# Hybrid decoder block on one core: the store of the last local attention outputs becomes a step of the latent attention's list scheduler

## The chip, the cores and the metric

The kernel runs on one core of one Trainium2 chip. Its engines are TensorE (PE, and PEld for its weight loads), VectorE (DVE), ScalarE (ACT), GpSimd (POOL) and SyncE (SP). SP only issues transfers here. The metric is the device time of one execution in microseconds; the time of a kernel is the median of its runs.

## The reference, cut to what matters

One layer over 1024 positions of width 1024, in float32:

```python
h = rmsnorm(x, mix_norm_g[l])
proj = h @ w_in[l]
qa, ka, va, q_lat, kv_lat, k_r, g_a, g_b = jnp.split(proj, IN_OFFSETS, axis=-1)
o_a = swa_sink_attention(qa, ka, va, swa_sinks[l])        # 8 heads, window of 128
cq = rmsnorm(q_lat, q_norm_g[l])                          # 384 wide
qb = (cq @ w_uq[l]).reshape(B, S, MLA_HEADS, MLA_QK_DIM)  # 64 plain + 32 rotary a head
ckv = rmsnorm(kv_lat, kv_norm_g[l])                       # 256 wide
kvb = (ckv @ w_ukv[l]).reshape(B, S, MLA_HEADS, MLA_NOPE_DIM + MLA_V_DIM)
o_b = mla_attention(q_nope, q_rope, k_nope, k_rope, vb)   # 8 heads, causal
y = jax.nn.sigmoid(g_a) * (o_a @ w_o_swa[l]) + jax.nn.sigmoid(g_b) * (o_b @ w_o_mla[l])
x = x + y @ w_out[l]
h = rmsnorm(x, ffn_norm_g[l])
x = x + (jax.nn.silu(h @ w_gate[l]) * (h @ w_up[l])) @ w_down[l]
```

A last norm follows.

## The kernel before

Positions are handled in 8 blocks of 128. Every float32 product is made of three matmuls on high and low halves: `mm3` (L263 to L269) multiplies high by high, high by low and low by high. So each operand is split first: ScalarE casts the high half (L260, or L1233 in the stage below), and DVE or POOL subtracts it for the low half (L261, L272).

The stages in order are: the projections; the local attention in 16 steps, with the products of the two gates between (class `Seven`, accumulators `fa` and `fb`); the opening of the latent attention (L1220 to L1457); the latent attention; the output mix; the feed-forward part. This change touches the joint between the local attention and the opening of the latent one.

**The end of the local attention.** `sw_pv(it)` (L1106) makes the output of one step and gathers four steps in a tile `oa` of 128 x 1024 floats (DVE, L1121 and L1122). After every fourth step, L1123 and L1124 store that tile to memory (`oa_d`, 512 KB), from where it is read again late in the latent attention (L1756). The last of the four stores comes from the call at L1203, the last line of the stage.

**The opening of the latent attention.** Its parts are steps of a list scheduler, class `Plan` (L95). A step has an engine, a cost, steps that it comes after, a rank, and the slots that it uses and frees. `run` (L110) keeps a clock for each engine, takes the step that can start first, with the lower rank ahead among those that can start within 30 ns, and emits its instructions; so the costs, ranks and slots set the order in which PE, DVE, ACT and POOL get their instructions. The steps that matter here:

- `c`, `k` (`latent_steps`, L1238): four transposes of the latents `lat` into a PSUM bank `lT`, then the high half (ACT) and the low half (DVE) into `cq` or `ckv`.
- `ld` (`load_steps`, L1295): loads of the raw weights, both parts of `w_uq` and both of `w_ukv`, in a tile `wr` each.
- `a` (`uq_steps`, L1303): the halves of the raw uq weights, in tiles `wuq`; `b` (`ukv_steps`): those of ukv, in `wv`.
- `r`, `ra`, `rj`, `rq`, `rd` (`rope_steps`, L1252): the rotary part of all queries, in two halves s of the positions. PE's product `r`, DVE's products with the tables `rope_cs`, POOL's joins `rr`, the halves `rq` (ACT, POOL) and the stores `rq_d` (L1280). `load_rope` (L1347) reads these rows back into the tiles `qT` of the heads (L1350).
- `x`, `xd`: the rotary keys (`krT`, then `kT`).
- `gm`, `ge` (`gate_steps`, L1352): the last products of the gates and the copies out of their banks; `gs` stores the gates (L1384).
- `Q`: the first query product; after it the latent attention starts, whose scores are `scb`.

The tiles `lat`, `wr`, `wuq`, `rr`, `go` and `oa` come from one pool, `u`, of 21 equal slots. The planner counts these slots: `in_use` (L1453) lists those taken when the opening starts, and each step's `use` and `free` take and return one. In the kernel before, `oa` is not in that list. Which buffer a tile then gets is decided by the pool when the step is emitted, and a tile put into a buffer waits, by semaphore, until the last reader of that buffer is done; for a buffer that a store reads, that is the landing of the store. PSUM banks (`p`, 4, and `w`, 4) are counted in the same way.

SP's queue holds all transfers of this stretch. A transfer whose wait isn't over holds up all behind it.

Of the kernel before, what the change touches and what calls it, by code (L numbers as in the profile page):

```python
# [18 lines left out]
S = 1024  # L19
D = 1024  # L20
NB = S // P
# [168 lines left out]
def hybrid_block_kernel(  # L190
# [29 lines left out]
    nc = tc.nc  # L220
# [23 lines left out]
    def U(name, dt=F32, shape=(P, 1024)):  # L244
        return pool.tile(list(shape), dt, tag="u", name=uid(name))
# [7 lines left out]
    def P1(name, shape=(P, 512)):  # L253
        return ps1.tile(list(shape), F32, tag="ps", name=uid(name))
# [22 lines left out]
    def blk(b, n=1):  # L277
        return slice(b * P, (b + n) * P)
# [27 lines left out]
    oa_d = dram.tile([4, P, 2, 512], F32, name="oa_d")  # L306
# [642 lines left out]
    oa_t = {}  # L949
# [156 lines left out]
    def sw_pv(it):  # L1106
        g, b = divmod(it, NB)
        d = sw.pop(it)
        po = P1("o", (P, 2, 2, P))
        prev = max(b - 1, 0)  # L1110
        steps = [(vv[prev // 4][:, prev % 4, g], 0)] + ([(vd[g][:, b], 1)] if b else [])
        for vst, n in steps:
            nc.tensor.matmul(po, vst, d["ph"][:, n], start=n == 0, stop=False)
            nc.tensor.matmul(po, vst, d["pl"][:, n], start=False, stop=n == len(steps) - 1)
        tmp = U("ot", F32, (P, 2, 2, P))
        nc.scalar.copy(tmp[0:64], po[64:128])
        if b % 4 == 0:
            oa_t[it // 4] = U("oa", F32, (P, 2, 512))
        oa = oa_t[it // 4]
        oc = blk(b % 4)  # L1120
        nc.vector.tensor_tensor(oa[0:64, :, oc], po[0:64, :, 0], tmp[0:64, :, 0], op=ALU.add)  # L1121
        nc.vector.tensor_tensor(oa[64:128, :, oc], po[0:64, :, 1], tmp[0:64, :, 1], op=ALU.add)  # L1122
        if b % 4 == 3:  # L1123
            nc.sync.dma_start(oa_d[it // 4], oa_t.pop(it // 4))  # L1124

    def kv_out(t, r, b):
# [42 lines left out]
    lat = []  # L1169
# [8 lines left out]
    for it in range(N_SW):  # L1178
        if it + 2 < N_SW:
            sw_q(it + 2)  # L1180
        gate_step()
        if it + 1 < N_SW:
            sw_qT(it + 1)
        if it in (0, 5):
            v_sums(it // 5)
        if it in (1, 6):
            v_parts(it // 6)
        gate_step()
        if it + 1 < N_SW:
            sw_scores(it + 1)  # L1190
        if it == N_SW - 1:
            st.load_to(st.index[("uq", 0)])
            load_lat(4)
        if it >= 1:
            sw_pv(it - 1)
        gate_step()
        sw_pT(it)
        if it + 1 < N_SW:
            sw_exp(it + 1)
    gate_step()  # L1200
    load_lat(NB)
    gate_step()
    sw_pv(N_SW - 1)  # L1203
    in_order.__exit__(None, None, None)

# [22 lines left out]
    def pre_step(kind, *key, x, **kw):  # L1228
        pre.add((kind, *key), rank=x + PRANK.get(kind, 0), **kw)
# [209 lines left out]
    for s in range(2):  # L1439
        pre_step("lf", s, x=0, eng="S", cost=1, emit=lambda: None, free=[("lat", 4 * s + b) for b in range(4)],  # L1440
                 after=[("c", j, s) for j in range(3)] + [("k", j, s) for j in range(2)] + [("x", s)])
    before = None
    for key, at in zip((("uq", 0), ("uq", 1), ("ukv", 0), ("ukv", 1)), XS["ld"]):
        load_steps(key, before, at)
# [5 lines left out]
    query_first_steps(XS["q"])  # L1450
    by_pre = tc.manual_schedule(engines={engines.PE, engines.DVE, engines.Activation, engines.Pool})
    by_pre.__enter__()
    in_use = [("lat", b) for b in range(NB)] + ["cos", "sin", ("graw", 0), ("graw", 1), "sum", "pu"]  # L1453
    in_use += [("gw", n) for n in GN if n < gates.n_prep]
    pre.run({"p": 4, "w": 4, "V": V_SLOTS, "U": U_SLOTS}, held=[("U", k, key) for k, key in enumerate(in_use)] + [("p", 3, ("gb", "A", 1))] + [
        ("V", 2 * n + i, ("hq", gates.seq[GN[n]][1], i)) for n in range(len(GN)) for i in range(2)])
# [945 lines left out]
```

## Time and profile before

| what | value |
|---|---|
| median of 3 runs | 1321.35 us (1320.81 to 1322.18) |
| the profiled execution | 1320.95 us |
| its span, first to last instruction | 1319.2 us |
| mean granted TensorE clock | 0.997 |
| moved by transfers | 210.49 MB, mean 160 GB/s |
| last stores of `oa` | issued at 316.40 us of the span |

The profile is one execution. Times in it are microseconds from the first instruction. A row of the timeline has the start, the length, the engine, the line, the operation, the tiles (out<-in), and in brackets the idle time of that engine ahead of it and what released it. "SPq" is SP issuing a transfer; its length is the time to issue it, not to move it. The busy table by stretch has for each engine the busy time and the number of instructions, then the granted clock, the share of the transfer engines' time and GB/s. The chain that ended last goes back from the last instruction, at each step to what released it.

### The profile page before, as it was taken

To read this page: it belongs to the slowest core of one execution; us is meant where nothing else is said; L and a number is where in the kernel's file an instruction comes from. 1 tells how busy PE (TensorE), PEld (TensorE's weight loads), DVE (VectorE), ACT (ScalarE), POOL (GpSimd) and SP (SyncE) were. 2 spreads that over 40 slices of the span, in tenths; PEclk is the share of its full clock that TensorE was granted. 3 is DMA by queue.
4 is the path that set the end of the run, shared out by engine and by line. 5 is a ranking of instruction groups with operands and counts; after the bars stand their busy time and mean duration, and the time that the engine had idled before them with its cause. 6 is when DMAs were issued, how large, how long until landed. Compare 5 with 4: busy or idle time off the path is not lost.

```text
span 1319.2 us, 18715 instructions
## 1 busy us (share of the span) xinstructions
PE 1306.1 (99%) x6463; PEld 1102.4 (84%) x6463; DVE 919.9 (70%) x1514; ACT 643.2 (49%) x1301; POOL 566.4 (43%) x552
## 2 busy tenths in 40 slices
PE   9999999999999999999999999999999999999997
PEld 6899888887888888888888888888888888888886
DVE  7869777765778885589889755766566555663962
ACT  7434666665477787545464322232223323644452
POOL 2116666553333267310134467775566621022520
PEclk9999999999999999999999999999999999999999
DMA  9454332436410022896231336743454335996503
GB/s 375 161 187 154 117 111 85 132 105 211 143 30 17 25 81 81 309 265 191 84 124 49 126 139 222 260 178 133 180 183 162 134 119 201 386 361 225 178 24 134
DMA packets 81246, 210.49 MB, mean 160 GB/s; under 512 B 9408, under 2 KB 16064, under 8 KB 80448
## 3 DMA queue, kind: packets, MB, share of 16 engines
q1 hardware_dynamic: 78416, 202.48, 43.4%
q0 software_dynamic: 1440, 4.72, 1.9%
q10 hardware_dynamic: 1296, 2.10, 0.5%
q8 instruction: 51, 0.84, 0.3%
q14 instruction: 43, 0.35, 0.1%
HBM read 143.34 MB, written 61.73 MB: 155 GB/s over the span
## 4 chain that ended last, share of the span: by engine, by line
PE 96%; DVE 1%; issue 1%; ACT 1%; DMA 1%; POOLq 0%; POOL 0%; SPq 0%; ACTq 0%; DVEq 0%
PE fa L269 8%; PE fa L267 8%; PE fa L268 8%; PE fb L267 6%; PE fb L269 6%; PE fb L268 6%; PE fd L268 5%; PE fd L267 5%; PE fd L269 5%; PE pTb L1580 2%; PE xo L268 2%; PE xo L267 2%; PE xo L269 2%; PE ob L1618 1%; PE scb L1535 1%; PE ob L1617 1%
## 5 line engine op out<-in xcount | busy, mean ns | idle before, releaser
L261 DVE TENSOR_TENSOR wl<-wr,wl 128x512 fp32r<-128x512 f32 x147 | 143.4, 997 | 67.6 <-ACT wl L260 67.2
L261 DVE TENSOR_TENSOR lrv<-lr,lrv 128x1024 fp32r<-128x1024 f32 x77 | 105.1, 1396 | 49.6 <-ACT lrv L260 48.2
L260 ACT CAST lrv<-lr 128x1024 fp32r<-128x1024 f32 x77 | 80.2, 1052 | 95.2 <-PE fd L269 70.7
L267 PE MATMUL fd<-lrv 128*128 128x512 f32 x308 | 119.8, 389 | 0.0
L268 PE MATMUL fd<-lrv 128*128 128x512 f32 x308 | 119.8, 389 | 0.0
L269 PE MATMUL fd<-lrv 128*128 128x512 f32 x308 | 119.8, 389 | 0.0
L260 ACT CAST wl<-wr 128x512 fp32r<-128x512 f32 x147 | 85.2, 620 | 3.6 <-DVE wr L962 1.7
L1564 POOL TENSOR_SCALAR p<-p,denb 128x384 f32<-128x384 f32 (+3 forms) x64 | 47.9, 750 | 86.8 <-DVE denb L1560 72.2
L261 DVE TENSOR_TENSOR wl<-sm,wl 128x512 fp32r<-128x512 f32 x59 | 52.1, 907 | 35.1 <-ACT wl L260 35.0
L275 POOL TENSOR_TENSOR wr<-wr,sm 128x512 f32<-128x512 f32 x20 | 30.5, 1529 | 97.5 <-DVE wl L261 97.5
L267 PEld LDWEIGHTS fd<-lrv 128*128 128x128 f32 x308 | 57.8, 188 | 12.1
L269 PEld LDWEIGHTS fd<-lrv 128*128 128x128 f32 x308 | 57.8, 188 | 12.0
L268 PEld LDWEIGHTS fd<-lrv 128*128 128x128 f32 x308 | 57.8, 188 | 11.9
L397 POOL TENSOR_SCALAR ms<-ss 128x1 f32<-128x1 f32 x32 | 10.4, 324 | 112.8 <-ACT xn L2131 62.8
L2043 ACT ACTIVATE act<-sm 128x512 f32<-128x512 f32 x11 | 7.0, 633 | 104.1 <-DVE sm L272 104.1
L272 DVE TENSOR_TENSOR ptl<-pTb,pth 128x512 fp32r<-128x512 f32 (+2 forms) x96 | 49.5, 548 | 8.7 <-ACT pth L1591 8.4
L275 POOL TENSOR_TENSOR sm<-wr,wr 128x512 f32<-128x512 f32 (+1 forms) x36 | 41.6, 1162 | 30.6 <-PE fb L269 26.1
L1555 ACT ACTIVATE p<-scb,nmb 128x384 f32<-128x384 f32 (+3 forms) x64 | 47.8, 748 | 13.0 <-DVE nmb L1550 9.0
L1550 DVE CUSTOM_DVE_ANT_0 scb<-scb,mask 128x384 f32<-128x384 f32 (+3 forms) x64 | 48.3, 760 | 6.9 <-PE scb L1537 6.3
L267 PE MATMUL fb<-t3h,wl 128*128 128x512 f32 x120 | 48.1, 401 | 0.0
L1591 ACT CAST pth<-pTb 128x512 fp32r<-128x512 f32 (+2 forms) x96 | 43.1, 484 | 9.9 <-PE pTb L1580 9.4
L268 PE MATMUL fb<-t3l,wl 128*128 128x512 f32 x120 | 47.4, 395 | 0.0
(403 smaller groups left out, 4258.1 us busy)
## 6 DMA issues: line engine op xcount, KB each, us to landing
lr<-la_d SPq DMA_DIRECT2D x77, 256.0 KB, 5.4
wr<-in_w_gate_dram SPq DMA_DIRECT2D x22, 512.0 KB, 4.4
wr<-in_w_up_dram SPq DMA_DIRECT2D x22, 512.0 KB, 5.1
la_d<-sd SPq DMA_DIRECT2D x22, 512.0 KB, 5.1
wd<-in_w_down_dram SPq DMA_DIRECT2D x22, 512.0 KB, 6.5
rb_d<-wd SPq DMA_DIRECT2D x22, 512.0 KB, 2.6
lr<-rb_d SPq DMA_DIRECT2D x44, 256.0 KB, 5.4
lr<-in_w_down_dram SPq DMA_DIRECT2D x33, 256.0 KB, 5.4
```

Of the source, the lines that this page charges most:

```text
L260: nc.scalar.copy(hi, src)
L261: (eng or nc.vector).tensor_tensor(lo, src, hi.bitcast(F32), op=ALU.subtract)
L267: nc.tensor.matmul(ps, ah, bh, start=first and i == 0, stop=False, skip_group_check=go_on)
L268: nc.tensor.matmul(ps, ah, bl, start=False, stop=False, skip_group_check=go_on)
L269: nc.tensor.matmul(ps, al, bh, start=False, stop=last and i == n - 1, skip_group_check=go_on)
L272: eng.tensor_tensor(out, a, b, op=ALU.subtract)
L275: eng.tensor_tensor(out, a, b, op=ALU.add)
L1550: nc.vector.tensor_tensor_reduce(s_, s_, m_, 1.0, -NEG, op0=ALU.add, op1=ALU.min, accum_out=nm)
L1555: nc.scalar.activation(p_, s_, AF.Exp, scale=-1.0, bias=t_.pop(("nm", key)), accum_out=den)
L1564: nc.gpsimd.tensor_scalar(p[:, 0:w], p[:, 0:w], den, 0.0, op0=ALU.mult, op1=ALU.add)
L1580: nc.tensor.transpose(pp[:, k], t_["p", key][:, blk(4 * g + k)], ident)
L1591: nc.scalar.copy(hi, pp)
```

## The change

```diff
@@ sw_pv
-        if b % 4 == 3:
+        if b % 4 == 3 and it < 2 * NB - 1:
             nc.sync.dma_start(oa_d[it // 4], oa_t.pop(it // 4))
@@ the steps of the opening
+    pre_step("of", x=12, eng="S", cost=5000, emit=lambda: nc.sync.dma_start(oa_d[3], oa_t.pop(3)), after=[("al", 0, 1)], free=("oa",))
     before = None
     for key, at in zip((("uq", 0), ("uq", 1), ("ukv", 0), ("ukv", 1)), XS["ld"]):
         load_steps(key, before, at)
@@ the slots taken at its start
-    in_use = [("lat", b) for b in range(NB)] + ["cos", "sin", ("graw", 0), ("graw", 1), "sum", "pu"]
+    in_use = [("lat", b) for b in range(NB)] + ["oa", "cos", "sin", ("graw", 0), ("graw", 1), "sum", "pu"]
```

The fourth store of `oa` is no longer issued where the tile is finished. It is a step `of` on SP that comes after the low half of the second uq tile (`al`, 0, 1), with a cost of 5 us to the planner, and it frees the slot `oa`, which counts as taken until then. The arithmetic is unchanged, and so is the number of instructions of each engine.

The step is a line of its own, L1442 of the kernel after, so everything behind it has a line number one higher there.

The rows that follow are the program's order with its waits. A wait `DMAHW5` is the landing of a transfer on lane 5: SP's transfers take eight lanes in turn, so that a transfer waits for the former one of its own lane too. The other names are the engines.

ScalarE, at the first copies of the opening, before (`lT` to `cq` are the latents, `wr_608` the raw uq weights, `go` the copy out of the gate's bank):

```order
L1233 CAST cq_638_3748<-lT_637_3743 128x512 [waits PE_49]
L1233 CAST wuq_644_3765<-wr_608_3607 128x384 [waits DMAHW7_49,DMAHW5_49,DMAHW0_49]
L1233 CAST cq_640_3755<-lT_639_3750 128x512 [waits PE_49]
L1233 CAST wuq_645_3782<-wr_608_3607 128x384 [waits DVE_49]
L1233 CAST cq_643_3764<-lT_642_3759 128x512 [waits PE_49]
L972 COPY go_647_3793<-fa_626_3683 128x512 [waits PE_49]
L1233 CAST cq_638_3748<-lT_646_3787 128x512 [waits PE_49]
L1233 CAST cq_640_3755<-lT_648_3796 128x512 [waits PE_49]
L1233 CAST cq_643_3764<-lT_650_3804 128x512 [waits PE_49]
```

and in the kernel after:

```order
L1233 CAST cq_638_3747<-lT_637_3742 128x512 [waits PE_49]
L1233 CAST wuq_644_3764<-wr_608_3607 128x384 [waits DMAHW0_49,DVE_49]
L1233 CAST cq_640_3754<-lT_639_3749 128x512 [waits PE_49]
L1233 CAST cq_643_3763<-lT_642_3758 128x512 [waits PE_49]
L1233 CAST wuq_646_3789<-wr_608_3607 128x384 [waits PE_49]
L1233 CAST cq_638_3747<-lT_645_3784 128x512 [waits PE_49]
L1233 CAST cq_640_3754<-lT_647_3791 128x512 [waits PE_49]
L1233 CAST cq_643_3763<-lT_648_3798 128x512 [waits PE_49]
L972 COPY go_651_3833<-fa_626_3683 128x512 [waits DVE_49]
```

The first `wuq` tile had the buffer of `oa` and waited for the store on lane 5; it now has another buffer, and waits for its own load (lane 0) and DVE. The second `wuq` moved back by one place, `go` by three, behind all copies of `cq`.

SP, at the store, before (`rope_cs` are the rotary tables, the first `wr` is the second part of uq, the others are ukv):

```order
L1219 DMA rope_cs_630_3710<-c_rope_t_dram 128x1024 [waits DMAHW4_49,PE_49]
L1124 DMA oa_d_89<-oa_576_3403 128x1024 [waits DVE_49]
L1219 DMA rope_cs_631_3711<-c_rope_t_dram 128x1024 [waits DMAHW6_49,PE_49]
L356 DMA wr_641_3757<-in_w_uq_dram 128x768 [waits DMAHW7_49,DVE_49]
L1384 DMA gate_d_88<-go_647_3793 128x512 [waits DMAHW0_49,Activation_49]
L376 DMA wr_649_3801<-in_w_ukv_dram 128x1024 [waits DMAHW1_49,DVE_49]
L376 DMA wr_654_3840<-in_w_ukv_dram 128x1024 [waits DMAHW2_49,PE_49]
```

and in the kernel after:

```order
L1219 DMA rope_cs_630_3709<-c_rope_t_dram 128x1024 [waits DMAHW4_49,PE_49]
L1219 DMA rope_cs_631_3710<-c_rope_t_dram 128x1024 [waits PE_49]
L356 DMA wr_641_3756<-in_w_uq_dram 128x768 [waits DMAHW6_49,DVE_49]
L1442 DMA oa_d_89<-oa_576_3403 128x1024 [waits DMAHW7_49]
L376 DMA wr_649_3818<-in_w_ukv_dram 128x1024 [waits DMAHW7_49,DMAHW0_49]
L1384 DMA gate_d_88<-go_651_3833 128x512 [waits DMAHW1_49,Activation_49]
L1384 DMA gate_d_88<-go_651_3833 128x512 [waits DMAHW2_49,DVE_49]
L376 DMA wr_661_3887<-in_w_ukv_dram 128x1024 [waits DMAHW6_49,DMAHW3_49,DVE_49]
```

The store moved behind the second table and the second part of uq. The first part of ukv now goes into the buffer of `oa` and waits for the store on lane 7. The second part of ukv waited for PE (the end of a gate product) and now waits for DVE, for the low half of the last `wuq`.

SP, at the stores of the rope rows, before (`rq_d` are the rows on their way to memory, `kT` the rotary keys, `qT` the rows read back):

```order
L1280 DMA rq_d_87<-rq_668_3929 256x1x512 [waits DMAHW4_49,Pool_49]
L1384 DMA gate_d_88<-go_670_3938 128x512 [waits DMAHW5_49,DVE_49]
L1280 DMA rq_d_87<-rq_668_3929 256x1x512 [waits DMAHW6_49]
L1344 DMA kT_673_3951<-kT_672_3950 32x2048 [waits DMAHW7_49,DVE_49]
L1344 DMA kT_674_3952<-kT_672_3950 32x2048 [waits DMAHW0_49]
L1350 DMA qT_679_4000<-rq_d_87 16x2x512 [waits DMAHW4_49,DMAHW1_49,PE_49]
```

and in the kernel after:

```order
L1384 DMA gate_d_88<-go_670_3935 128x512 [waits DMAHW4_49,DVE_49]
L1280 DMA rq_d_87<-rq_668_3927 256x1x512 [waits DMAHW5_49,Pool_49]
L1280 DMA rq_d_87<-rq_668_3927 256x1x512
L1344 DMA kT_673_3950<-kT_672_3949 32x2048 [waits DVE_49]
L1344 DMA kT_674_3951<-kT_672_3949 32x2048 [waits DMAHW0_49,PE_49]
L1350 DMA qT_679_4001<-rq_d_87 16x2x512 [waits DMAHW5_49,DMAHW1_49,PE_49]
```

The gate store moved ahead of the two stores of the rope rows, which stand next to each other now.

## The prediction

> **What bounds the kernel now.** First the page, for the span and the busiest engine.
>
> ```profile
> span 1319.2 us, 18715 instructions
> PE 1306.1 (99%) x6463; PEld 1102.4 (84%) x6463; DVE 919.9 (70%) x1514; ACT 643.2 (49%) x1301; POOL 566.4 (43%) x552
> ```
>
> TensorE is busy in 1306.1 of 1319.2 us, so only time in which it waits or runs slowly can be won by a reordering. The step from the local attention to the latent attention, where the change sits, has both kinds, as the busy time by stretch (PE's share first, then the granted clock and DMA at the end) shows.
>
> ```profile
> 322.00:324.00 2.00, 0.06 (x1) 0.00 (x0) 1.49 (x3) 2.00 (x6) 0.00 (x0) 1.00 0.17 66
> 325.00:328.00 3.00, 3.00 (x9) 2.38 (x8) 1.66 (x3) 0.86 (x2) 0.00 (x0) 0.50 0.76 246
> 329.00:332.00 3.00, 3.00 (x15) 2.48 (x14) 1.89 (x3) 0.75 (x2) 0.00 (x0) 1.00 0.48 160
> ```
>
> From 322 to 324 TensorE does nothing; from 325 to 328 it is busy at half the clock (0.50), nine matmuls where 329 to 332 has fifteen. The chain that ended last, in order of time, names the cause.
>
> ```profile
> 316.40 2.46 DMA oa_d<-oa
> 318.86 2.76 issue
> 321.62 0.51 ACT wuq L1233
> 322.14 0.49 ACT cq L1233
> ...
> 323.52 0.50 ACT go L972
> ```
>
> ScalarE finished its transposed block at 318.86 and then stood still for 2.76 us. "Issue" means that the profile names no engine for it, but the chain comes from the store of oa, and the landing times of that stretch fit:
>
> ```profile
> wr<-in_w_ukv_dram SPq DMA_DIRECT2D x2, 512.0 KB, 3.4
> oa_d<-oa SPq DMA_DIRECT2D x1, 512.0 KB, 5.2
> wr<-in_w_uq_dram SPq DMA_DIRECT2D x1, 384.0 KB, 6.5
> ```
>
> The store was issued at 316.40 and took 5.2: it landed at 321.60, and the cast wuq began at 321.62. The cast writes the buffer out of which the store was still reading (its wait list has the store's lane). Behind it in ScalarE's order stand the copies cq and the copy go, and for go, which empties a PSUM bank, TensorE's transposes wait:
>
> ```profile
> 317.38 1.47 PE L1243 MATMUL lT<-ident,lat 128*128 128x128 f32 x12
> 318.61 0.48 PE L267 MATMUL fa<-hh,wl 128*128 128x512 f32 x1
> ...
> 321.46 0.60 PE L1243 MATMUL lT<-ident,lat 128*128 128x128 f32 x4
> 324.06 1.18 PE L1243 MATMUL lT<-ident,lat 128*128 128x128 f32 x8 [2.00 <-ACT go L972]
> 324.91 0.76 PE L267 MATMUL fb<-t3h,wl 128*128 128x512 f32 x1
> ...
> 329.35 0.39 PE L267 MATMUL r<-cq,wuq 128*128 128x512 f32 x1
> ```
>
> **What the change removes.** The planner now holds oa's slot, so the first wuq goes to the buffer of a spent gate weight, and its wait list has the landing of its own load and DVE's last low half wl instead of the store. That low half and what DVE does next are here:
>
> ```profile
> 317.62 1.36 DVE L272 TENSOR_TENSOR wl<-wr,wl 128x512 fp32r<-128x512 f32 x2
> ...
> 319.49 0.68 DVE L272 TENSOR_TENSOR cq<-lT,cq 128x512 fp32r<-128x512 f32 x1
> ...
> 322.17 0.56 DVE L272 TENSOR_TENSOR wuq<-wr,wuq 128x384 fp32r<-128x384 f32 x1 [1.99 <-ACT wuq L1233]
> ```
>
> The low half ends at 318.98, so wuq can start at about 319.0 instead of 321.62, and the two cq copies follow at 319.5 and 320.0. DVE then does wuq (0.56) and two cq (0.68 each) by 321.9. The four transposes at 321.46 and the eight behind them need those cq lows and no longer the copy go, which moved behind all six cq. TensorE reaches the last group at about 322.3, after 321.9: no wait is left. Twelve transposes take 318.61 - 317.38 = 1.23 us, so fb starts at 321.46 + 1.23 = 322.69 instead of 324.91: **2.22 us**.
>
> fb's twelve matmuls took 329.35 - 324.91 = 4.44 us; fa's twelve at full clock took 321.46 - 318.61 = 2.85. If the half clock came from the idle gap, it goes with it: **1.59 us**. The clock is 1.00 still in the gap, 0.50 right behind it, and 1.00 again from 329 on, which is why I count it. [...]
>
> Together 3.81 us at the first r product, which would start at 325.54.
>
> **What it adds and moves.** The same 512 KB store is issued, once; nothing is added but its place. On SP's queue it now stands behind both rope tables and the second load of uq, which before stood behind it: those go out up to 1.5 us earlier, the store at about 317.6. The load of ukv's first part takes oa's slot and waits for the store's landing, with two gate stores behind it. In the old trace all four transfers had landed by 317.29 + 6.5 = 323.8 (uq is the last; its issue is below); with the same bytes issued no later, 323.8 is my bound, and the load goes out by then instead of at 324.45. I cost this at nothing: it lands by 327.4 (3.6 after its issue), and its casts and lows are done by about 330.6, when DVE is wanted for go. Every microsecond past that would delay what follows.
>
> The second part of ukv is where something is late next. It moved from SP's place behind fb to behind the second pair of wuq lows on DVE. From 325.54 TensorE does r (nine matmuls at 2.85 / 12, 2.1 us) and fa (2.85), which ends at 330.5. Then DVE does go, wuq, a rope product and wuq (0.7 for those of the shape of cq, 0.6 for wuq, and some 0.5 for ScalarE's cast between), so the load is issued at 333.7 and lands 3.4 later at 337.1. The casts and the rope halves are priced from these rows:
>
> ```profile
> 317.29 0.38 SPq L356 DMA_DIRECT2D wr<-in_w_uq_dram  x1
> 324.45 0.38 SPq L376 DMA_DIRECT2D wr<-in_w_ukv_dram  x1
> 332.76 1.14 ACT L1233 CAST wv<-wr 128x512 fp32r<-128x512 f32 x2 [0.77 <-DMA wr<-in_w_ukv_dram]
> 340.11 1.05 ACT L1233 CAST rq<-rr 128x1024 fp32r<-128x1024 f32 x1 [0.19 <-POOL rr L275]
> 341.23 2.39 POOL L272 TENSOR_TENSOR rq<-rr,rq 128x1024 fp32r<-128x1024 f32 x1 [1.16 <-ACT rq L1233]
> ```
>
> Two casts end at 338.2, the rope cast at 339.3, the next copy ckv at 339.8 and its low half on DVE at 340.5. TensorE wants that bank for the second krT at 340.5 as well. Bounds: nothing to 0.6 us if the load lands half a microsecond later; I take **0.3 given back**.
>
> POOL's low half of the rope rows ends at 341.7 (341.23 + 2.39 = 343.62 before: 1.9 earlier, where TensorE is 3.8 earlier). So the road of the rope rows to memory and back is the narrow place:
>
> ```profile
> 343.65 0.63 SPq L1280 DMA_DIRECT2D rq_d<-rq  x1
> 344.98 1.98 SPq L1280 DMA_DIRECT2D rq_d<-rq  x1
> 350.59 0.57 SPq L1350 DMA_DIRECT2D qT<-rq_d  x1
> 352.53 0.58 SPq L1280 DMA_DIRECT2D rq_d<-rq  x1
> 357.29 0.58 SPq L1350 DMA_DIRECT2D qT<-rq_d  x1
> qT<-rq_d SPq DMA_DIRECT2D x1, 64.0 KB, 2.5
> 359.42 0.39 PE L269 MATMUL v<-wv,ckv 128*128 128x512 f32 x1
> 359.90 0.47 PE L1535 MATMUL scb<-kT,qT 96*128 96x512 f32 x1
> ```
>
> The last load of rows, issued at 357.29, landed 2.5 later at 359.79, and the score scb began at 359.90 where 359.65 was its turn: TensorE already touches this road. First store pair to the second load took 350.59 - 343.65 = 6.94 us, with a gate store between the two; the later pair, with nothing between, took 357.29 - 352.53 = 4.76. The change puts that gate store ahead of the pair. Nearest is therefore 4.76; 6.94 is the far end. From 341.7: + 4.76 = 346.5, + 1.94 to the next store = 348.4, + 4.76 = 353.2, + 2.61 to the score = 355.8. TensorE itself comes at 359.65 - 3.81 + 0.3 = 356.1, so the road is just free. With 6.94 for the first pair the score begins at 358.0.
>
> **The sum.** 3.81 less 0.3 is 3.5 us. The stages behind have the same order on TensorE, and I find no other wait there that a later start would have covered. The profiled execution took 1320.95 (span 1319.2 and 1.75 around it): 1317.45. It stood 0.4 under the median of the runs, 1321.35, so the forecast for a median is **1317.8**, 0.27% less. About 0.2%, 2.6 us, is what a measurement of this kernel can tell from no change: faster means under 1318.7, slower over 1324.0.
>
> **The rivals.**
> - *The rope rows become the bound.* For it: the score at 359.90 is released by their landing now, and they gain 1.9 us where TensorE gains 3.8. Against it: the second pair is fast without a store in between. At the far end the score starts at 358.0, 1.9 us saved: 1319.4, within 0.2%.
> - *The half clock stays*, because it has another cause than the gap. For it: 2.0 us is a short gap. Against it: the clock is 1.00 on both sides of that stretch, and nothing but the gap stands at its start. Then 2.22 is saved, less 0.3: 1319.4. [...]
> - *The wait only changes its name.* ScalarE would wait for DVE or the uq load as long as for the store. Against it: DVE's row ends at 318.98, and that load is much older than the store. Price: 0 to 1 us saved, 1320.9.
> - *Slower: the store, pushed back, holds up ukv.* Through oa's slot both ukv parts follow its landing. If it landed d us after 323.8, the second krT and the rope rows would move by up to d. It decides from d = 3.8, a landing 10 us after issue, where the longest of that stretch is 6.5; at d = 6.5 and with a new gap's half clock (1.6) the time is 1321.35 + 2.7 + 1.6 = 1325.7.
>
> **How the numbers follow.** The forecast gets 0.62 (2.7 to 4.1 saved, the upper end being 3.81 and the 0.25 at the score), the rope rows 0.16, the clock 0.06, the wait renamed 0.11, slower 0.05. Faster by over 0.2% is the forecast and a little of the rope rows, 0.64; slower 0.05; within it the rest, 0.31. The forecast's own range is 1317.2 to 1318.7. The range for 8 in 10 goes from 1316.9 to 1320.2: it takes in the rope rows, the clock and half of the renamed wait.
>
> **What would show it.** Right: the first wuq on ScalarE at about 319.0 with no wait ahead of it; transposes on TensorE in one run of twelve from 321.4; fb at 0.23 us a matmul and a clock of 1.00; r at 325.5; the score behind v at 356. Wrong: a gap on TensorE ahead of the second krT (ukv late) or ahead of the first or third score (rope rows), or fb still at 0.43 us a matmul without a gap. If the first r comes at 325.5 and the end is still less than 2.6 us earlier, the loss stands between those two places.

## The result, and the profile after

| | before | after |
|---|---|---|
| median of 20 runs each (range) | 1320.61 us (1318.80 to 1323.19) | 1318.88 us (1318.11 to 1320.49) |
| ratio after / before, 95% interval | | 0.9985, 0.9979 to 0.9991 |
| the profiled execution, and its span | 1320.95, 1319.2 | 1318.39, 1316.7 |

The kernel is 1.73 us faster by the medians, 0.13% (0.15% by the ratio, 0.09 to 0.21%), where 3.5 us were forecast. The two profiled executions differ by 2.56. The interval leaves out 1, so the gain is told from no change, though it is smaller than the 0.2% that the prediction took as its limit. One execution of a later experiment (rows_and_order) ran at a mean clock of 0.556 (2194.95 us); it is left out of all counts and medians below.

The page of the changed kernel, span and busiest engine:

```profile
span 1316.7 us, 18714 instructions
PE 1304.8 (99%) x6463; PEld 1101.2 (84%) x6463; DVE 926.5 (70%) x1514; ACT 642.4 (49%) x1301; POOL 567.3 (43%) x552
```

The busy time by stretch, at the place of the old gap and of the old half clock:

```profile
322.00:324.00 2.00, 2.00 (x16) 1.87 (x15) 1.89 (x5) 1.76 (x4) 0.00 (x0) 1.00 0.08 33
325.00:328.00 3.00, 3.00 (x15) 2.48 (x14) 0.87 (x2) 0.00 (x0) 0.00 (x0) 1.00 0.87 249
```

TensorE works through both stretches at a clock of 1.00: fifteen matmuls from 325 to 328, where before had nine. The timeline of ScalarE shows why:

```profile
318.94 0.59 ACT L1233 CAST cq<-lT 128x512 fp32r<-128x512 f32 x1
319.84 0.51 ACT L1233 CAST wuq<-wr 128x384 fp32r<-128x384 f32 x1 [0.32 <-DVE wl L272]
320.26 1.07 ACT L1233 CAST cq<-lT 128x512 fp32r<-128x512 f32 x2
322.24 0.51 ACT L1233 CAST wuq<-wr 128x384 fp32r<-128x384 f32 x1 [0.91 <-PE fa L269]
322.68 1.56 ACT L1233 CAST cq<-lT 128x512 fp32r<-128x512 f32 x3
324.11 0.62 ACT L972 COPY go<-fa 128x512 f32<-128x512 f32 x1
```

The first wuq waits 0.32 for VectorE's low half wl instead of 2.76 for the store, and go stands behind all six cq. On TensorE, in the timeline:

```profile
317.96 1.47 PE L1243 MATMUL lT<-ident,lat 128*128 128x128 f32 x12
...
322.04 1.47 PE L1243 MATMUL lT<-ident,lat 128*128 128x128 f32 x12
323.27 0.48 PE L267 MATMUL fb<-t3h,wl 128*128 128x512 f32 x1
...
326.12 0.39 PE L267 MATMUL r<-cq,wuq 128*128 128x512 f32 x1
...
341.10 0.60 PE L1330 MATMUL krT<-ident,lat 128*32 128x128 f32 x4
...
352.23 0.44 PE L1538 MATMUL scb<-kT,qT 96*128 96x384 f32 x1 [0.36 <-DVE qT L1412]
...
357.40 0.47 PE L1536 MATMUL scb<-kT,qT 96*128 96x512 f32 x1 [0.58 <-DMA qT<-rq_d]
```

The first lT comes 0.58 us later in this execution than in the old one (317.38), for reasons far ahead of the joint: in part a wait of 0.34 for a transfer at 117.57 that the old one has not, while the rest was not traced. In five executions of before it lies anywhere from 317.36 to 318.23. So from here on times count **from the first lT**. Counted so, fb starts 2.22 us earlier than before (5.31 against 7.53), the first r 3.81 (8.16 against 11.97), the second krT 3.86, and the third score only 3.08 (39.44 against 42.52). From the third score to the end both spans take 959.3 us. This pair thus gains 3.81 us at the joint, loses a net 0.7 at two waits ahead of the third score, and shows 3.08 - 0.58 = 2.5 in the span.

### The profile page after: what moved, and what is told of

It reads as the page before. It is cut to its first block, busy times and chain, and to the rows that moved or that the text cites. A ratio compares the mean times of both kernels' runs of the same rounds, so it can differ in the third digit from the quotient of the medians.

```text
span 1316.7 us, 18714 instructions
## 1 busy us (share of the span) xinstructions
PE 1304.8 (99%) x6463; PEld 1101.2 (84%) x6463; DVE 926.5 (70%) x1514; ACT 642.4 (49%) x1301; POOL 567.3 (43%) x552
## 4 chain that ended last, share of the span: by engine, by line
PE 89%; DVE 4%; DMA 2%; issue 2%; ACT 1%; POOL 1%; SPq 0%; POOLq 0%; DVEq 0%; ACTq 0%
PE fa L267 8%; PE fa L269 8%; PE fa L268 8%; PE fb L269 6%; PE fb L267 6%; PE fb L268 6%; PE fd L268 5%; PE fd L267 5%; PE fd L269 5%; PE pTb L1581 2%; PE xo L267 2%; PE xo L269 2%; PE xo L268 2%; PE ob L1619 1%; PE scb L1536 1%
## 5 line engine op out<-in xcount | busy, mean ns | idle before, releaser
L261 DVE TENSOR_TENSOR wl<-sm,wl 128x512 fp32r<-128x512 f32 x59 | 55.6, 966 | 34.8 <-ACT wl L260 34.6
L267 PE MATMUL fb<-t2h,wl 128*128 128x512 f32 x120 | 47.1, 393 | 0.0
```

The costliest lines, as they stand in the source:

```text
L261: (eng or nc.vector).tensor_tensor(lo, src, hi.bitcast(F32), op=ALU.subtract)
L267: nc.tensor.matmul(ps, ah, bh, start=first and i == 0, stop=False, skip_group_check=go_on)
```

## The experiments

**The kernel before, four more times.** No edit. Does one profiled execution stand for all?

> The kernel before, unchanged. What is read: the time from the first transpose lT of the joint to the first product r (11.97 us in the first profile of before), the idle gap ahead of the second lT run (2.00) and the twelve matmuls of fb behind it (4.44 at half clock, 2.85 at full). Theory A (the gap always brings the half clock; the missing 1.5 us of the gain is scatter ahead of the joint): again 11.8 to 12.2, fb 4.3 to 4.5, and the runs scatter over some 4 us as they did. Theory B (the half clock comes in some executions only): a fair chance that fb takes 2.8 to 3.0 with a gap of 2.0 still there, and r at 10.2 to 10.6. By both the ratio to before is 1.000 within 0.0006.

> The kernel before, unchanged, one more profiled execution. Theory (the landing of the store scatters from one execution to the next, and the half clock comes only where the gap is near 2 us or more): wait of ScalarE for the landing anywhere from 0.5 to 3.5 us, gap on TensorE from 0 to 2.7; with a gap under 1.1 fb takes 2.85 and r comes at 9 to 10 after the first lT, with one of 2 or more some 1.6 us are lost to the half clock and r comes at 11.9 to 12.7. The time of this execution goes with it: under 1320 in the first case, 1321 to 1323 in the second. Rival (landing and gap are always as in the two profiles so far): gap 2.0 to 2.7, whatever the time.

> The same as before_2, one more profiled execution, with the same two expectations.

> The kernel before, one more profiled execution. Theory: gap on TensorE 1.8 to 2.8; either fb takes 2.85, r comes at 10.2 to 11.0 after the first lT and the time is under 1321, or 1.5 to 1.7 us go to the half clock, r comes at 11.8 to 12.8 and the time is 1320.9 to 1323.2. Rival (the time of an execution does not go with its clock behind the gap): the other pairing.

The results, with both executions of the changed kernel beside them:

| execution | time us | store's landing after issue | gap on TensorE | twelve fb | first r | third score |
|---|---|---|---|---|---|---|
| before | 1320.95 | 5.2 | 2.00 | 4.44 | 11.97 | 42.52 |
| before_again | 1322.36 | 5.9 | 2.71 | 3.67 | 12.68 | 43.44 |
| before_2 | 1322.12 | 5.1 | 1.95 | 4.42 | 11.90 | 42.38 |
| before_3 | 1320.49 | 5.1 | 1.91 | 2.85 | 10.29 | 41.18 |
| before_4 | 1319.17 | 5.0 | 1.82 | 2.85 | 10.20 | 40.87 |
| after | 1318.39 | 6.0 | none | 2.85 | 8.16 | 39.44 |
| after_again | 1318.26 | 5.8 | none | 2.85 | 8.16 | 39.45 |

The gap is in every profiled execution of before, 1.8 to 2.7 us, and it is the store's landing that sets it. The half clock is not in every one. The rows of before_2 and before_3 side by side (a row of the timeline each, then busy time by stretch; the clock is the third number from the end):

```profile
324.86 1.09 PE L1243 MATMUL lT<-ident,lat 128*128 128x128 f32 x8 [1.95 <-ACT go L972]
...
326.00:327.00 1.00, 1.00 (x4) 0.78 (x3) 1.00 (x3) 0.63 (x2) 0.00 (x0) 0.55 1.02 289
327.00:328.00 1.00, 1.00 (x4) 0.80 (x3) 0.46 (x1) 0.00 (x0) 0.00 (x0) 0.50 0.89 328
328.00:329.00 1.00, 1.00 (x4) 0.71 (x3) 0.00 (x0) 0.21 (x1) 0.00 (x0) 0.50 0.13 49
329.00:330.00 1.00, 1.00 (x5) 0.81 (x4) 0.00 (x0) 0.93 (x2) 0.00 (x0) 0.75 0.00 0
```

```profile
324.45 1.09 PE L1243 MATMUL lT<-ident,lat 128*128 128x128 f32 x8 [1.91 <-ACT go L972]
...
326.00:327.00 1.00, 1.00 (x6) 0.79 (x5) 1.00 (x2) 0.22 (x1) 0.00 (x0) 1.00 1.00 315
327.00:328.00 1.00, 1.00 (x6) 0.83 (x5) 0.05 (x1) 0.00 (x0) 0.00 (x0) 1.00 0.52 197
```

Behind a gap of 1.95 TensorE does four matmuls a microsecond at a clock of 0.50, behind one of 1.91 six at 1.00. What before_2 expected, that the landing scatters by microseconds, did not show: it takes 5.0 to 5.9 us. The half clock does stand with the longer gaps, but 1.91 and 1.95 differ by 0.04 us; what else differs between these executions was not shown. The 11 times of before_again fall into two groups, four from 1319.55 to 1320.44 and seven from 1322.24 to 1322.95.

**The planner's new order without the buffer (plan_only).** All four engines get the changed kernel's order; only the buffer of the first wuq and the store's place are as before.

```diff
-        if b % 4 == 3 and it < 2 * NB - 1:
-            nc.sync.dma_start(oa_d[it // 4], oa_t.pop(it // 4))
+        if b % 4 == 3:
+            nc.sync.dma_start(oa_d[it // 4], oa_t.pop(it // 4) if it < 2 * NB - 1 else oa_t[3])
...
-    pre_step("of", ..., emit=lambda: nc.sync.dma_start(oa_d[3], oa_t.pop(3)), ...)
+    pre_step("of", ..., emit=lambda: oa_t.pop(3), ...)
```

> The planner's new order without the changed buffer: the planner holds the slot, but the store is issued where it was and the first wuq is again put into the buffer that the store is still reading. Theory (the wait for the store's landing is the cause): the wuq cast still begins when the store has landed, some 2.6 us after ScalarE came free; only the copy go has left its place ahead of the cq copies, worth 0.5 us at most; r at 11.2 to 12.0 after the first lT, and a time within 0.1% of before (1319.3 to 1321.3 where before has 1320.6). Rival (the new order of the steps brings the gain, the buffer does not): r at 8.2, ratio 0.9985.

Measured: 1320.90, ratio to before 0.9997 (0.9988 to 1.0006). ScalarE and TensorE in its timeline, the last row the third score:

```profile
321.13 0.51 ACT L1233 CAST wuq<-wr 128x384 fp32r<-128x384 f32 x1 [1.92 <-issue]
...
322.90 1.25 PE L1243 MATMUL lT<-ident,lat 128*128 128x128 f32 x8 [1.04 <-DVE cq L272]
...
358.43 0.47 PE L1536 MATMUL scb<-kT,qT 96*128 96x512 f32 x1 [0.97 <-DMA qT<-rq_d]
```

The wait stays: the store, issued at 316.20, lands 4.9 later and the cast starts at once. In this execution the gap is 1.04, fb's matmuls start 0.23 or 0.24 us apart, as they do at a clock of 1.00, and the first r comes at 9.59, earlier than expected, since go no longer stands in the way. But the third score, which waits 0.97 for the rope rows, comes at 41.24, no earlier than in before_3 and before_4 (41.18 and 40.87), and the time is before's: the new order does not bring the gain.

**The slot alone (hold_slot).** As plan_only, but the buffer is kept by one row of 4 KB that the planner's step stores once more; the 512 KB are stored at the old place.

```diff
-    pre_step("of", ..., emit=lambda: oa_t.pop(3), ...)
+    pre_step("of", ..., emit=lambda: nc.sync.dma_start(oa_d[3][0:1], oa_t.pop(3)[0:1]), ...)
```

> The slot alone: the store of 512 KB is issued where it was before (ahead of the second rope table and uq), and the buffer is kept until the planner's step, which only stores one row of 4 KB once more. Theory (the buffer is all of it, the store's new place does nothing): r at 8.1 to 8.3 after the first lT, no gap, full clock, time as the changed kernel's, 1318.4 to 1319.4. Rival (the new place of the store carries part of the gain, because uq and the rope table go ahead of it): more than 0.5 us behind the changed kernel, 1319.5 or more.

Measured: 1318.63, ratio 0.9980 (0.9971 to 0.9989); the first r at 8.15. ScalarE again:

```profile
319.37 0.51 ACT L1233 CAST wuq<-wr 128x384 fp32r<-128x384 f32 x1
319.79 1.07 ACT L1233 CAST cq<-lT 128x512 fp32r<-128x512 f32 x2
```

The cast starts at 319.37, while the store, issued at 316.76, lands only 5.5 later. With the same order as plan_only and the same early store, the other buffer takes the wait away and brings the whole gain: the medians of the two, timed side by side, are 2.27 us apart. That the store moves makes no difference that shows.

**The store alone (late_store).** It is issued behind both rope tables, and no slot is held.

```diff
-        if b % 4 == 3:
+        if b % 4 == 3 and it < 2 * NB - 1:
...
+    pre_step("of", x=-30, eng="S", cost=400, emit=lambda: nc.sync.dma_start(oa_d[3], oa_t.pop(3)))
```

> The store alone: it is issued behind both rope tables, as in the changed kernel, but the slot is not held, so a wuq cast (now the second) again waits for its landing. Theory (the wait for the landing is the cause, at 1 us for 1 us): the store lands 1 to 2.5 us later than before, the gap on TensorE grows from 2.0 to 3.0 to 4.5, r at 13 to 14.6 after the first lT, and the time is 1 to 2.6 us over before, 1321.6 to 1323.2. Rival (the landing is not what the cast waits for): gap and time as before, 1320.6 within 0.6.

Measured: 1321.89, ratio 1.0003 (0.9993 to 1.0012), gap 2.05, first r at 12.01, fb's matmuls 0.43 us apart, as they are at half clock. From its timeline:

```profile
316.88 0.33 SPq L1442 DMA_DIRECT2D oa_d<-oa  x1
...
323.06 0.51 ACT L1233 CAST wuq<-wr 128x384 fp32r<-128x384 f32 x1 [2.81 <-DMA oa_d<-oa]
```

Here the profile names the store itself as what ended ScalarE's wait (6.2 after its issue). Counted from the first lT it lands 1.0 later than in before, but the gap did not grow as expected: the wait went to the second wuq, with the first wuq and one cq done ahead of it, and that took up the later landing. The price of a longer gap was therefore not measured here. The table has one: before_again, with a gap 0.71 longer than before's, has its first r 0.71 later.

**The gap filled (fill_gap).** Five repeats of the four transposes ahead of the gap, which write the same values again.

```diff
-            for b in range(4):
+            for b in list(range(4)) * (6 if (kind, j, s) == ("c", 0, 1) else 1):
```

> The kernel before with five repeats of the four transposes ahead of the gap (20 transposes, 2.1 us of TensorE, which write the same values to the same bank): the wait for the store stays, but TensorE is busy in it. Theory (the idle gap brings the half clock): fb at full clock, 2.85 for its twelve matmuls, r at 10.0 to 10.9 after the first lT where the gap was 2.0 to 2.7; the slow half of the executions goes, so the highest time falls from 1323.5 to about 1322 and the median by 0.3 to 1.0 us (ratio 0.9993 to 0.9998). Rival (the half clock has another cause): fb 4.4, r at 12 or later, ratio 1.000 or more.

Measured: 1320.17 (1319.82 to 1321.43), ratio 1.0000 (0.9991 to 1.0009); before, timed beside it, 1320.14 (1318.74 to 1323.02). TensorE in its timeline, and busy time by stretch:

```profile
322.00 3.65 PE L1243 MATMUL lT<-ident,lat 128*128 128x128 f32 x32
325.40 0.48 PE L267 MATMUL fb<-t3h,wl 128*128 128x512 f32 x1
...
325.00:328.00 3.00, 3.00 (x17) 2.56 (x16) 1.89 (x3) 1.38 (x3) 0.00 (x0) 1.00 0.80 255
```

fb starts as late as in before_2 (7.48) but runs at full clock, and r comes at 10.34 instead of 11.90. The filling was not free in it: go was done 6.17 after the first lT against 6.58 in before_2, since the store landed after 4.7 instead of 5.1, so without the filling fb could have started some 0.4 earlier (an estimate from these two). None of the 11 executions passes 1321.43; of before, 33 of 117 do, but only 2 of the 21 that were timed beside fill_gap, so the times add little to the profile. The expected fall of the median failed, and the lowest time rose by 1.1: 9 of those 21 lie below it. Executions whose gap is shorter than the filling must pay for the rest of it, as this one did by 0.4; one that pays 1.1 was not profiled, so that part stays open.

**The rope rows (rows_early).** In the changed kernel, the second pair of stores ahead of the loads of the second head's rows.

```diff
-            for h in (0, 1):
-                load_rope(h, 0)
+            load_rope(0, 0)
...
+        pre_step("R", 1, x=x - 1, eng="S", cost=1500, emit=lambda: load_rope(1, 0), after=[("R", 0), ("rd", 1)])
```

> The changed kernel, with the rope rows of the second half stored ahead of the loads of the second head's first rows, instead of behind them: SyncE issues that pair 1.2 us earlier. Theory (after the change the road of the rope rows holds up the third score by 0.6 to 0.9 us): the wait ahead of that score goes or falls under 0.1, it starts at 38.7 to 38.9 after the first lT (39.44 in the changed kernel), and the time is 0.5 to 0.9 under the changed kernel's: 1318.0 to 1318.4, ratio to before 0.9978 to 0.9982. Rival (the loads, not the stores' issue, set the landing): the wait stays, time as the changed kernel's.

What was to be mended stands in SP's timeline of the changed kernel:

```profile
342.15 2.56 SPq L1280 DMA_DIRECT2D rq_d<-rq  x2
344.76 1.47 SPq L1344 DMA_DIRECT2D kT<-kT  x2
346.34 3.79 SPq L1350 DMA_DIRECT2D qT<-rq_d  x4
350.19 1.25 SPq L1280 DMA_DIRECT2D rq_d<-rq  x2
```

POOL is done with the second half's rows at 348.61 (its low half starts at 346.20 and takes 2.41), but SP is in the four loads until 350.13. In rows_early:

```profile
345.22 2.56 SPq L1350 DMA_DIRECT2D qT<-rq_d  x2
348.09 1.24 SPq L1280 DMA_DIRECT2D rq_d<-rq  x2
...
356.19 0.40 PE L1536 MATMUL scb<-kT,qT 96*128 96x512 f32 x1
```

The third score has no wait any more and comes at 38.93 instead of 39.44, though this execution's r came 0.24 later. The time, 1318.51 (ratio 0.9987, 0.9978 to 0.9996), cannot be told from the changed kernel's; the expected 0.5 to 0.9 us were not to be seen in it.

**The changed kernel again, and two versions past it.** rows_and_order adds one fixed order for the steps of both plans:

```diff
-    by_pre.__exit__(None, None, None)
...
-    by_plan = tc.manual_schedule(engines={engines.PE, engines.DVE, engines.Activation, engines.Pool})
-    by_plan.__enter__()
...
-    by_plan.__exit__(None, None, None)
+    by_pre.__exit__(None, None, None)
```

early_store is this with hold_slot's store.

> The changed kernel, unchanged, a second profiled execution and a second timing, as the neighbour of the next two. Theory (before loses its gap in every execution and the half clock in some; the changed kernel never has either): second run of twelve lT without a gap, fb 2.85, r at 8.1 to 8.5 after the first lT, third score held up 0.5 to 0.9 us by the rope rows; no run over 1321; median 1318.4 to 1319.2, ratio to before 0.9982 to 0.9990. Rival (the changed kernel has slow executions of its own, which the first timing shows as its runs over 1320): a gap or a half clock in this profile, or runs over 1321.

> The changed kernel with the earlier rope rows of rows_early, and the steps of both plans in one fixed order, so that VectorE does the first query's low halves ahead of the first key's (qT, qT, kT, kT instead of kT, kT, qT, qT). Theory: the wait of 0.36 us ahead of the first score's third matmul goes as well; the first score runs in one piece, the third starts at 38.2 to 38.5 after the first lT if the rope rows have landed by then, else at 38.9; time 0.3 to 0.5 under rows_early, 0.7 to 1.3 under the changed kernel of the same call. Rival (the next wait, for the rope rows, takes it back): first score in one piece, third score waits, time as rows_early, 0.4 to 0.8 under the changed kernel.

> As rows_and_order, with the store issued at its old place and only the slot held to the planner's step (as in hold_slot). Theory (the place of the store does nothing for TensorE): the same as rows_and_order within 0.4 us. Rival (an earlier store clears the queue for what follows): lower by more than 0.4 us.

Measured side by side, before at 1320.28: after_again 1318.97, ratio 0.9987 (0.9978 to 0.9996), highest 1319.31; rows_and_order 1318.32, 0.9980 (0.9971 to 0.9990); early_store 1318.14, 0.9982 (0.9974 to 0.9991). VectorE and TensorE of rows_and_order:

```profile
348.27 1.39 DVE L1412 SCALAR_TENSOR_TENSOR qT<-q,qT 64x512 fp32r<-64x512 f32 x2 [0.88 <-ACT qT L1416]
349.69 1.41 DVE L272 TENSOR_TENSOR kT<-k,kT 64x512 fp32r<-64x512 f32 x2
...
351.27 0.34 PE L1537 MATMUL scb<-kT,qT 96*128 96x384 f32 x1
...
356.06 0.47 PE L1535 MATMUL scb<-kT,qT 96*128 96x512 f32 x1 [0.33 <-DMA qT<-rq_d]
```

The first score runs in one piece and the third comes at 38.54, 0.91 earlier than in after_again, with 0.33 of waiting for the rope rows again, as the rival had it. The medians are 0.65 and 0.83 lower than the changed kernel's; the intervals overlap, so the trace shows the gain and the times only fit it. The store's place again made no difference that shows. The profiled execution of early_store is the highest of its twelve, 1320.33: its first lT came at 319.72, later than in any other profile, and its third score at 38.77 from there.

## Why the prediction was right, and where its size was off

**The cause: right.** The wait was for the landing of the store, through the buffer. plan_only and hold_slot differ in nothing that TensorE, VectorE, ScalarE or POOL do in order, and have the two times. The first r of the changed kernel comes at 8.16 from the first lT, where 325.54 - 317.38 = 8.16 was forecast.

**2.22 us at fb: right** to the hundredth for the profiled pair, and 2.04 to 2.13 at r against before_3 and before_4, whose gaps were a little shorter.

**1.59 us of half clock: this term was mis-sized.** "If the half clock came from the idle gap, it goes with it" holds in every execution without a gap that was profiled (fb takes 2.84 to 2.86 in all seven). But the forecast counted the whole of it for a median, from one execution. Of five profiled executions of before three have it and two do not, at gaps of 1.95 to 2.71 and of 1.82 to 1.91. The times only bound its share: of 117 timed ones 33, or 28%, lie above 1321.43, the highest of fill_gap, and 55, or 47%, above 1320.49, the highest of the 76 of the kernels that have no gap (the first profile of before has the half clock at 1320.95). In the executions without it the changed kernel gains 1.43 to 1.74 us at the third score (40.87 and 41.18 less 39.44), and the medians, 1.73 apart in the first comparison and 1.31 in the second, have that size. That a median of before is one without the half clock fits both bounds, but is not shown execution by execution. The rival "the half clock stays" had this size, 1319.4, for another reason, and lies nearer to the measured 1318.88 than the forecast does.

Why only some executions have it was not shown. The seven executions that were profiled with a gap at this place are these; the clock is the lowest in a stretch of 1 us from 324 to 330, and where none stands, the distance of fb's matmuls (0.42 or 0.43 us at a clock of 0.50, 0.23 or 0.24 at 1.00) tells it:

| execution | gap on TensorE | its length | clock behind it | third to fourth matmul of fb |
|---|---|---|---|---|
| before | 322.06 to 324.06 | 2.00 | 0.50 | 0.43 |
| before_again | 322.21 to 324.92 | 2.71 | 0.50 | 0.42 |
| before_2 | 322.91 to 324.86 | 1.95 | 0.50 | 0.43 |
| late_store | 322.54 to 324.59 | 2.05 | | 0.43 |
| before_3 | 322.54 to 324.45 | 1.91 | 1.00 | 0.23 |
| before_4 | 322.04 to 323.86 | 1.82 | 1.00 | 0.24 |
| plan_only | 321.86 to 322.90 | 1.04 | | 0.24 |

Added up over the stretches, the half clock lasts 3.4 us in before, before_again and before_2 (in before_2 0.55, 0.50, 0.50 and 0.75 from 326 to 330: 0.9 + 2 + 0.5). It begins some 0.9 us behind the gap's end in before, at once in before_again and some 1.2 us behind it in before_2. The four gaps of 1.95 us or more have it and the three of 1.91 or less do not, but these two figures lie 0.04 us apart, and no profiled gap lies between them.

That idleness brings the fall, and not the wait for the store as such, fits fill_gap: ScalarE's wait stays (2.05), TensorE is busy in it, and the clock stays at 1.00. But it stays at 1.00 in two of the five executions of before as well, so this one execution does not decide it.

**ukv costing nothing: right.** The first part was issued at 324.19, which less the 0.58 is 323.61 in the old trace's count; the bound was 323.8. **0.3 given back by its second part: wrong by a little.** It was issued at 334.30 less 0.58 = 333.72, as forecast (333.7), and the second krT did not wait.

**The rope rows "just free": wrong, and the rival of them came half true.** The prediction named a gap ahead of the first or third score as a sign that it was wrong, and both came, the one at the first score from VectorE (below). POOL's half ended at 342.12 (339.73 and 2.39 long), less 0.58 = 341.54, where 341.7 was forecast. But from the first pair of stores to the second SP took 350.19 - 342.15 = 8.04, where the forecast had 4.76 + 1.94 = 6.70: the later pair, from which 4.76 was taken, has no kT transfers between store and load, and the first pair has two (1.47). The third score waited 0.58.

**Not forecast:** VectorE's order at the first score turned from kT, qT, qT, kT to kT, kT, qT, qT, and the third matmul waited 0.36 for it. The first rows are before's, from the chain that ended last; the others are the changed kernel's timeline.

```profile
353.30 0.68 DVE kT L272
353.98 0.60 DVE qT L1412
354.61 0.70 DVE qT L1412
```

```profile
350.05 1.41 DVE L272 TENSOR_TENSOR kT<-k,kT 64x512 fp32r<-64x512 f32 x2 [2.13 <-ACT kT L1702]
351.49 1.41 DVE L1412 SCALAR_TENSOR_TENSOR qT<-q,qT 64x512 fp32r<-64x512 f32 x2
```

With the rope rows this takes 0.7 us in the first pair, where 0.3 was written off.

**The base.** The forecast started from a median of three, 1321.35; that of 20 was 1320.61. The error of the time (1318.88 against 1317.8) is smaller than that of the gain (1.73 against 3.5, half of it) for this reason, and that is luck. The time lies in the wide range (1316.9 to 1320.2), but not in the forecast's own (1317.2 to 1318.7): the likeliest outcome, with the chance of 0.62, did not come, and the gain of 0.15% lies within the 0.2% that had the chance of 0.31.

## What to carry to other kernels

The buffer that the store reads was taken until the store had landed (in before the landing is at 321.60, the cast into the buffer at 321.62). Where a planner frees such a buffer when the store is issued, look for an engine that stands still for it with all that is queued behind, as ScalarE did for 2.76 us; the profile may show the wait only as "issue", as it did there. Before a stall's after-effect is counted in full, profile the kernel two or three times: what one execution shows at its full size may be missing in others, as the half clock was in two of the five profiles of before. When a stall goes, look along the whole road to the next meeting of engines with its own transfers counted, not those of a similar pair.

## What the runs showed of the hardware

TensorE's clock fell to 0.50 for 3.4 us behind idle gaps of 2.00, 2.71 and 1.95 us (before, before_again, before_2); behind one of 2.05 in late_store fb's matmuls were 0.43 us apart, as in those three (0.42 or 0.43). It stayed at 1.00 behind gaps of 1.91 and 1.82 (before_3, before_4), and behind one of 1.04 in plan_only the matmuls were 0.23 or 0.24 apart. With twenty more transposes in the wait it stayed at 1.00 in the profiled execution of fill_gap, at a cost of some 0.4 us there (the estimate above). The same 512 KB store took 4.7 to 6.7 us to land across the fourteen profiles.
